# A decoder step on one core: state products in four row ranges, feed-forward without marking products, another closing chain, and new constants for the planner

## The chip, the cores and the metric

The kernel runs on one core of a Trainium2 chip, as one launch. The metric is the device time of that launch in microseconds (us); lower is better. The engines named below are TensorE (PE: matrix products; PEld is its weight load), VectorE (DVE), ScalarE (ACT), GpSimd (POOL) and SyncE (SP, which only issues DMAs). PE writes its products into PSUM, of which the kernel uses eight banks of 128 partitions by 512 fp32 values; its other tiles are in SBUF.

## The reference

One decoder layer is computed for 512 prompt tokens and for 8 x 4 sample tokens that share all weights; the kernel holds both as one block of N = 544 columns. In short:

```python
h = rmsnorm(x, norm_mix); z = h @ w_in            # attention q,k,v and HGRN q,f,i,g
f = lb + (1 - lb) * sigmoid(hf); qh = silu(hq) * HG_DK**-0.5
# HGRN, 4 heads of 128 x 128 state, causal; S0 = 0 for the prompt, given for each of the 8 samples
S_t = diag(f_t) S_{t-1} + (1 - f_t) outer i_t;  o_t = S_t^T qh_t
x = x + concat(att, o_normed_and_gated) @ w_out
x = x + cross_attention(rmsnorm(x)) @ w_co
u = rmsnorm(x, norm_ffn)
x = x + (silu(conv3(u @ w_gate)) * (u @ w_up)) @ w_down
y = rmsnorm(x, norm_final)
```

The outputs are y for prompt and samples, the new k and v rows, the HGRN states after the step, the last two gate rows and the memory keys and values.

## The kernel before, in words

**Numbers as pairs.** Nearly every large product runs on fp32r operands split into a high and a low part, three products for one (high x high, high x low, low x high). ACT makes the high parts, DVE the low ones. Small products (transposes, the HGRN state work, sums over partitions) stay in fp32, and each of those shows as two PE records.

**The recorder.** The kernel isn't issued as it is written. `Tape` records every call as a step with an estimated length (`_Engine.take`), its tiles and what it depends on; `Tape.order` then plays all engines forward in time and writes one fixed order for each engine. Steps recorded under `tape.main()` are the big products: they keep their written order on PE. All other PE work is side work, which the planner puts between them in bursts. The class constants (`BURST`, `PATIENCE`, `NEAR`, `SLACK`, `LEAD`, `MARGIN` and so on) say how eager it is, `EVEN` stretches the due times. Tiles of one kind share a pool (`a`: 71 SBUF tiles); a step can only be placed once its pool has room. The planner only orders instructions; on the chip nothing of it runs.

**PSUM.** Two banks are `dense` (`PD`), five are `aux` (`PX`), one is `dec` (`PDEC`); `PF` takes PD, PD, PDEC in turn.

**Stages, as the trace shows them.** Input projections and HGRN/attention as side work up to 307 us; output projection (`ps_wo`) to 355; cross attention to 428; feed-forward from 428 to about 730; the last third of the down projection (`ps_dz`, `ps_az`, `ps_cz`, `ps_ez`) to 786; closing norm and output after that.

**An HGRN head** (`hgrn`). `by_token_s` turns the 32 sample rows of v (into `psA`) and k (into `psin`) by a 128 x 32 product with the identity; two such copies go to partitions 0-31 and 32-63. ACT copies them to `hsm` (64 x 128). POOL spreads v into `hvm` (64 x 4 x 128), with `batch` as a mask. Two products with 32 rows and 512 columns, in two row ranges and two aux banks (`psu`), give the state updates of samples 0-3 and 4-7; eight DVE operations add each 128 x 128 part to the decayed state `hst`, which a DMA stores. `psU` and `psin` are aux banks that live around it; `pso` is the head's output, read by ACT as `ho`, normed, and used as `om` in the output projection.

**Feed-forward.** The gate and up projections run as `PLAIN` tiles (two gate, two up, columns cut 256 + 288 by `CUTS`) and then as 20 `Pair` units (Strassen/Winograd: seven products of 272 columns for two tiles, banks `a`, `c`, `d`). After product 1, ACT copies bank `a` into bank `d` (`keep`), and product 2 accumulates onto the copy. Before that, `mark_banks` (5 products) and `mark_down` (3 products) write 272 columns of each bank once. Products follow in the order 1, 3 of the unit before, 2, 6, 7, 4 of the unit before, 5; product 3 accumulates onto bank `a` after the copy `r` of product 5 has been read (`keptu` in the trace).

**Closing.** `last_half(7, 1)` makes the last 256 columns of the last feature tile: 30 products into `ps_dz`, a DVE add of `ps_dz` to x (`xr`), an ACT square (`sq_last`), then `final(1)`: sums over partitions (`psr_final`), ACT Ln (`r_fin`) and Exp (`r_final`), 8 scalings for each column cut (DVE or POOL) and 8 output DMAs for each, on SP for the first cut, on SP and ACT in turn for the second.

**Start.** The first DMAs are issued in written order: `vec` (norm weights) on ACT's queue; on SP's queue the first 256 columns of x, the first weights `wf[0]` in two pieces, the other columns of x, then x and weights in turn.

Of the kernel before, what the change touches and what calls it, by code (L numbers as in the profile page):

```python
# [12 lines left out]
AF = mybir.ActivationFunctionType  # L13
# [6 lines left out]
TS = 4  # L20
# [52 lines left out]
LAST_CUTS = ((0, 288), (288, 256))  # L73

# [21 lines left out]
for _n, _c in (("ident", 128), ("ones", 128), ("blk64", 128), ("dbias", NR + 2 * NS),  # L96
               ("mask_a", 96), ("mask_b", 96), ("mask_s", 96), ("batch", 4), ("sel32", 32), ("own", 2)):
    _span(CST_COLS, _n, _c)
# [17 lines left out]
def _constants():  # L116

    c = np.zeros((128, NCST), np.float32)

    def put(name, a):  # L120
        lo, hi = CST_COLS[name]
        c[:a.shape[0], lo:hi] = a.reshape(a.shape[0], hi - lo)

    p = np.arange(128)
    put("ident", np.eye(128))
    put("ones", np.ones((128, 128)))
    put("blk64", (p[:, None] // 64 == p[None, :] // 64).astype(np.float32))
# [27 lines left out]
    put("batch", ((p[:64, None] % 32 // TS) == 4 * (p[:64, None] // 32) + np.arange(4)[None, :]).astype(np.float32))  # L155
# [114 lines left out]
class Tape:  # L270
# [185 lines left out]
    def order(self):  # L456
# [16 lines left out]
        takes = sorted(takes.items(), key=lambda t: t[1])  # L473
        waiting = {e: [] for e in ("PE", "ACT", "DVE", "POOL", "SP")}
# [84 lines left out]
        def start(s):  # L559
            nonlocal todo, bus, mode  # L560
            waiting[s.engine].remove(s)
            for k, v in needs(s).items():
                room[k] -= v
            for n in s.tiles:
                if n in last and n not in held:
                    ends[n] = last[n]
# [19 lines left out]
            if s.main:  # L586
                clock[:] = s.est, now
            for n in s.tiles:
                if n in self.kinds:
                    left[n] -= 1  # L590
                    if not left[n]:
                        ends.pop(n, None)
                        frees.append((s.end + s.lag, self.kinds[n]))
# [70 lines left out]
class _Engine:  # L664
# [5 lines left out]
    def __getattr__(self, method):  # L670
# [3 lines left out]
        def take(*args, **kw):  # L674
# [10 lines left out]
            if engine == "PE":  # L685
                n, m, k = int(np.prod(args[2].shape[1:])), outs[0].shape[0], args[1].shape[0]
                codes = 2 if method == "transpose" or args[1].dtype == F32R else 4
                if method == "transpose":
                    n, length = 128, 0.11
                elif args[1].dtype == F32R:  # L690
                    length = 0.000456 * n + 0.001
                else:
                    least = 0.112 if m == 128 and k == 128 else 0.0105
                    length = 2 * max(least, 0.00086 * n * (max(m, 128 - 2 * k) / 128 if m < 128 else 1.0) * (0.59 if k <= 64 else 1.0))
                    length *= 0.5 if k <= 32 and m <= 32 else 1.0
# [3 lines left out]
            elif engine == "ACT":  # L699
                length = 0.05 + 0.00086 * n + 0.19 * ("accum_out" in kw)  # L700
                if hasattr(kw.get("bias"), "ap") or hasattr(kw.get("scale"), "ap"):
                    length += 0.13
# [6 lines left out]
            else:  # L709
                port = method == "tensor_tensor"  # L710
                length = {"tensor_tensor": 0.2 + 0.0026 * n, "memset": 0.15 + 0.0007 * n,
                          "tensor_scalar": 0.2 + 0.0036 * n}.get(method, 0.45 + 0.0009 * n)
# [5 lines left out]
def tile_decoder_step(ctx: ExitStack, tc: tile.TileContext, xT, memT, kwT, vw, s0, conv_in, mkT, mv, vecs, cst,  # L718
# [42 lines left out]
    nc.scalar.dma_start(vec[:, :KT], vecs[:, :KT])  # L761
# [158 lines left out]
    def passes(ps, w, xs, n0, n, order, first=True, last=True):  # L920
        for at, i in enumerate(order):
            (hi, lo), (xh, xl) = w[i], xs[i]
            for j, (a, b) in enumerate(((hi, xh), (hi, xl), (lo, xh))):
                nc.tensor.matmul(ps[:, :n], a, b[:, n0:n0 + n], start=(first and at == 0 and j == 0),
                                 stop=(last and at == len(order) - 1 and j == 2))
# [541 lines left out]
    def hgrn(h, f, q, gt, v):  # L1467
# [44 lines left out]
        def level_products(w, kq):  # L1512
# [8 lines left out]
            elif w == 32:  # L1521
                bank["l"] = PX(f"psL{h}")
                for c in range(4):
                    for j in (0, 64):
                        t0 = 128 * c + j
                        nc.tensor.matmul(bank["l"][j:j + 32, 128 * c + j + 32:128 * c + j + 64], kq[:, t0:t0 + 32],
                                         kq[:, t0 + 32:t0 + 64], start=True, stop=True)
            else:
                for c in range(4):
                    t0 = 128 * c  # L1530
                    nc.tensor.matmul(bank["l"][0:64, t0 + 64:t0 + 128], kq[:, t0:t0 + 64], kq[:, t0 + 64:t0 + 128],
                                     start=True, stop=True)

# [16 lines left out]
        vs, ks, ats = sml[:2 * NS, 0:128], sml[:2 * NS, 128:256], sml[:NS, 256:352]  # L1550
# [7 lines left out]
        for i in range(2):  # L1558

            by_token_s(v, bank["a"][NS * i:NS * i + NS, 384:512])  # L1560
# [11 lines left out]
        nc.scalar.copy(vs, bank["a"][:2 * NS, 384:512])  # L1572
# [8 lines left out]
        for i in range(2):  # L1581
            by_token_s(k, pin[NS * i:NS * i + NS, 256:384])
# [7 lines left out]
        nc.scalar.copy(ks, pin[:2 * NS, 256:384])  # L1590
        nc.vector.tensor_tensor(tmp[:, :384], tmp[:, :384], tmp2[:, :384], op=ALU.add)
        vm = A(f"hvm{h}", [128, 4, 128])
        nc.gpsimd.tensor_tensor(vm[:2 * NS], vs[:, None, :].to_broadcast([2 * NS, 4, 128]),
                                C("batch")[:2 * NS, :, None].to_broadcast([2 * NS, 4, 128]), op=ALU.mult)
# [8 lines left out]
        U, pus = PX(f"psU{h}"), [PX(f"psu{h}{i}") for i in range(2)]  # L1603
# [541 lines left out]
    def plain_tile(kind, j, i):  # L2145
# [9 lines left out]
        for cut in CUTS:  # L2155
# [200 lines left out]
    class Pair:  # L2356


        def __init__(self, kind, j, gates):
            self.name, self.w, self.s, self.low = f"{kind}{j}", {"A11": {}, "A12": {}}, {}, {}  # L2360
            src = w_gate if kind == "g" else w_up

# [47 lines left out]
        def product(self, bank, a, b, first, *deps):  # L2410
            def fn():
# [3 lines left out]
                for k in range(4):  # L2415
                    (hi, lo), (xh, xl) = w[k], xs[k]
                    for i, (l, r) in enumerate(((hi, xh), (hi, xl), (lo, xh))):
                        nc.tensor.matmul(ps[:, :HT], l, r, start=first and k == 0 and i == 0, stop=k == 3 and i == 2,
                                         skip_group_check=True)
            return later.pe(fn, self.low[a], tok_low[b, 0], tok_low[b, 1], *deps)  # L2420

        def keep(self, name, q):
            def fn():
                if name == "q":
                    out = self.s["d"] = PX(f"ps_d{self.name}")
# [48 lines left out]
    def mark_banks():  # L2474


        for i in range(5):
            nc.tensor.matmul(PX(f"ps_mark{i}")[:, :HT], ux[0][0][:, :128], ux[0][0][:, :HT], start=True, stop=True)

    later.pe(mark_banks)  # L2480
    later.pe(lambda: ffn_in.rows(1))
    seq[1:1] = [later.order.pop(), later.order.pop()]
    before = None

    def mark_down():

        for ps in (PD("ps_mark_a"), PD("ps_mark_d"), PDEC("ps_mark_c")):
            nc.tensor.matmul(ps[:, :HT], b_side("B11")[0][0][:, :128], b_side("B11")[0][0], start=True, stop=True)
# [33 lines left out]
    def last_half(m, c):  # L2522
# [309 lines left out]
```

## Time and profile before

| what | value |
|---|---|
| median of 3 runs | 799.51 us (799.26 to 799.98) |
| profiled execution | 798.79 us |
| its span, first to last instruction | 797.0 us |
| granted TensorE clock | 0.996 |
| PE busy | 784.1 us (98%), 7440 products |
| DVE / ACT / POOL busy | 673.9 / 480.1 / 206.6 us |
| HBM traffic | 142.9 MB (134.80 read, 8.07 written) |

The profiled execution's own time is 1.8 us above its span, and 0.7 us below the median of the runs. A PE record lasts from issue to the end of the pipeline, so records overlap: the time that a product costs is read from its start to the start of the next one, not from its duration.

### The profile page before, as it was taken

Reading aid. Unit: us, or ns where it says so; the run is one execution under the profiler, and the core shown is the slowest. Engines: PE = TensorE matmul, PEld = TensorE weight load, DVE = VectorE, ACT = ScalarE, POOL = GpSimd, SP = SyncE. Lnnn points to the kernel's source line nnn. Section 1 sums busy time; section 2 is a strip of 40 time slices with the busy share of each in tenths; the row PEclk is TensorE's granted clock in tenths of the full one; section 3 lists DMA queues with packets and bytes.
Section 4 is the critical chain, followed back from the end, with each engine's and each line's share of the span. In section 5 each row is a group of like instructions: output and inputs, shape, how many; then the busy total and the mean of one; then the engine's idle time right before and its main releaser. Section 6 shows DMA issues by size and latency. Waiting matters only on the chain.

```text
span 797.0 us, 19226 instructions
## 1 busy us (share of the span) xinstructions
PE 784.1 (98%) x7440; PEld 742.0 (93%) x7440; DVE 673.9 (85%) x1507; ACT 480.1 (60%) x1040; POOL 206.6 (26%) x284
## 2 busy tenths in 40 slices
PE   9999999999999999999999999999999999999995
PEld 9998878887898989999999999999999999999994
DVE  6889888578978886674888999999999998989963
ACT  8724468826558545553685767656665766567642
POOL 1131200030211110231234337423532433232023
PEclk9999999999999999999999999999999999999998
DMA  9753897799652364441754467877968877786103
GB/s 306 260 147 103 282 322 223 261 353 305 207 203 80 109 215 153 132 147 52 255 165 119 83 173 177 188 177 199 186 159 192 204 160 186 185 240 158 52 1 112
DMA packets 107419, 144.12 MB, mean 181 GB/s; under 512 B 7360, under 2 KB 73920, under 8 KB 107328
## 3 DMA queue, kind: packets, MB, share of 16 engines
q1 hardware_dynamic: 91728, 124.01, 48.3%
q0 software_dynamic: 14880, 18.36, 14.5%
q8 instruction: 58, 0.95, 0.5%
q10 hardware_dynamic: 720, 0.53, 0.2%
q14 instruction: 33, 0.27, 0.1%
HBM read 134.80 MB, written 8.07 MB: 179 GB/s over the span
## 4 chain that ended last, share of the span: by engine, by line
PE 97%; ACT 1%; DVE 1%; issue 0%; DVEq 0%; ACTq 0%
PE ps_ag L713 7%; PE ps_au L713 7%; PE ps_wo L713 6%; PE ps_aw L713 5%; PE ps_cu L713 4%; PE ps_cg L713 4%; PE ps_q L713 3%; PE ps_co L713 3%; PE ps_cq L713 3%; PE ps_first L713 3%; PE ps_dz L713 3%; PE ps_az L713 3%; PE ps_hv L713 2%; PE ps_cw L713 2%; PE ps_dg L713 2%; PE ps_ck L713 2%
## 5 line engine op out<-in xcount | busy, mean ns | idle before, releaser
L713 DVE TENSOR_TENSOR wl<-wr,wh 128x512 fp32r<-128x512 f32 x98 | 69.5, 733 | 3.3 <-ACT wh L713 3.2
L713 ACT CAST wh<-wr 128x512 fp32r<-128x512 f32 x98 | 56.3, 618 | 11.9 <-DMA wr<-in_w_in 6.1
L713 POOL TENSOR_TENSOR hG<-hG,hf 128x256 f32<-128x256 f32 (+1 forms) x28 | 25.1, 897 | 134.4 <-DVE hf L713 79.5
L713 POOL COPY last<-ug 128x2 f32<-128x2 f32 (+1 forms) x44 | 31.9, 788 | 59.0 <-DVE ug L713 56.4
L713 DVE SCALAR_TENSOR_TENSOR cv<-ug,vec,cv 128x560 f32<-128x560 f32 x44 | 35.2, 800 | 1.6 <-ACT cv L713 1.1
L684 POOL DMA_DIRECT2D S13w<-in_w_down x12 | 12.2, 1013 | 61.3 <-DVE ug L713 8.3
L713 POOL TENSOR_TENSOR acc_cx<-acc_cx,sq_cx 128x256 f32<-128x256 f32 (+1 forms) x14 | 12.6, 904 | 56.7 <-PE ps_wo L713 30.7
L713 ACT COPY keptg<-ps_ag 128x272 f32<-128x272 f32 x20 | 7.7, 386 | 28.9 <-PE ps_ag L713 28.9
L713 ACT ACTIVATE cv<-ug,vec 128x560 f32<-128x560 f32 x22 | 18.9, 858 | 4.7 <-POOL ug L713 3.5
L713 DVE TENSOR_TENSOR xr<-xr,ps_wo 128x256 f32<-128x256 f32 (+1 forms) x16 | 6.8, 436 | 15.1 <-PE ps_wo L713 15.1
L713 ACT ACTIVATE cv<-cv 128x560 f32<-128x560 f32 x22 | 14.8, 671 | 7.7 <-DVE cv L713 7.5
L713 PE MATMUL ps_co<-coh,wh 128*128 128x256 f32 (+1 forms) x64 | 19.0, 297 | 0.0
L713 POOL TENSOR_TENSOR acc_final<-acc_final,sq_final 128x256 f32<-128x256 f32 (+1 forms) x10 | 8.2, 834 | 40.2 <-ACT sq_final L713 40.1
L713 PE MATMUL ps_co<-coh,wl 128*128 128x256 f32 (+1 forms) x64 | 18.4, 288 | 0.0
L713 PE MATMUL ps_co<-col,wh 128*128 128x256 f32 (+1 forms) x64 | 18.4, 288 | 0.0
L713 POOL COPY ug<-conv_state 128x16 f32<-128x16 f32 x22 | 17.9, 992 | 0.0
L713 ACT ACTIVATE P<-P,mx 128x128 f32<-128x128 f32 (+3 forms) x32 | 17.6, 553 | 0.2
L713 ACT COPY hsm<-psA 64x128 f32<-64x128 f32 x4 | 1.0, 258 | 26.0 <-PE psA L713 17.7
L713 POOL MEMSET hG<- 128x544 f32 x4 | 2.2, 550 | 56.0 <-PE psr_att L713 45.9
L713 DVE TENSOR_TENSOR xr<-xr,ps_aw 128x272 f32<-128x272 f32 x36 | 15.6, 433 | 0.8 <-PE ps_aw L713 0.5
L713 DVE TENSOR_TENSOR hf<-hf 128x256 f32<-128x256 f32 (+1 forms) x28 | 12.2, 435 | 4.8 <-POOL hG L713 4.5
L713 PE MATMUL psd<-st,qbd_win 128*32 128x224 f32 x256 | 16.0, 358 | 0.0
(3348 smaller groups left out, 3812.7 us busy)
## 6 DMA issues: line engine op xcount, KB each, us to landing
st<-in_kwT SPq DMA_DIRECT2D x32, 448.0 KB, 5.6
st<-in_vw SPq DMA_DIRECT2D x28, 512.0 KB, 5.5
wr<-in_w_in SPq DMA_DIRECT2D x25, 512.0 KB, 6.6
wrg<-in_w_gate SPq DMA_DIRECT2D x10, 512.0 KB, 5.7
wru<-in_w_up SPq DMA_DIRECT2D x10, 512.0 KB, 4.8
st<-in_mkT SPq DMA_DIRECT2D x8, 512.0 KB, 5.4
wr<-in_w_out SPq DMA_DIRECT2D x8, 512.0 KB, 3.7
S13w<-in_w_down SPq DMA_DIRECT2D x24, 128.0 KB, 3.2
```

The source lines that it names most:

```text
L684: return tape.put(engine, lambda: call(*args, **kw), outs, ins, 0.1, 0.3, size)
L713: return tape.put(engine, lambda: call(*args, **kw), outs, ins, length, lag, size, port, codes, work, mode)
```

## The change

**State update of a head.** `by_token_s` runs four times for v and four times for k, into four 32-row ranges; `hsm`'s parts become 128 x 128, the mask `batch` has two columns, and POOL writes `hvm` as 128 x 2 x 128. Four products of 32 rows and 256 columns, in four row ranges and four aux banks, take the place of two of 512. The DVE work stays, reading other banks.

**Feed-forward.** Both marking steps go. The first three units write bank `d` once with one product at the end of product 1, and the last two plain tiles are cut 272 + 272. In the last unit product 7 goes behind product 5.

**Closing.** For the last feature tile ACT copies x into the PSUM bank ahead of the products, which accumulate onto it; ACT squares the bank directly, and DVE copies it to x.

**Start.** `wf[0]` goes to ACT's queue ahead of the table load; `vec` goes to SP's queue behind the first piece of x.

**Recorder.** New constants and lengths, and the planner now hands out a bank of a pool in the order in which banks are given back.

```diff
+HALVES = ((0, N // 2), (N // 2, N // 2))
+MARKED = 3
...
-    ROUNDS, EVEN = 2, 1.013
+    ROUNDS, EVEN = 2, 1.017
-    SWITCH, NEAR = 0.14, 3.9
-    SPELL, ACTIVE, IDLE, COLD = 3.4, 0.45, 0.45, 2.0
-    BURST, PATIENCE, SLACK, LEAD, MARGIN = 1.75, 3.7, 16.5, 15.95, 4.95
+    SWITCH, NEAR = 0.16, 3.25
+    SPELL, ACTIVE, IDLE, COLD = 3.4, 0.46, 0.45, 2.0
+    BURST, PATIENCE, SLACK, LEAD, MARGIN = 1.9, 5.85, 15.65, 14.75, 3.65
...
-            return all(room[k] >= v for k, v in want.items()) and ("a" not in want or leaves_room(s, want["a"]))
+            return all(room[k] >= v if k == "a" else len(give[k]) >= v and max(give[k][:v]) <= now + 1e-9
+                       for k, v in want.items()) and ("a" not in want or leaves_room(s, want["a"]))
...
-    nc.scalar.dma_start(vec[:, :KT], vecs[:, :KT])
...
+        for c0, c1 in ((0, 128), (128, 384)):
+            nc.scalar.dma_start(wf[0][:, c0:c1], w_first[0][:, c0:c1])
         nc.scalar.preload_act_table_set(LN_SET)
         x_load(0, 0, 256)
-        for c0, c1 in ((0, 128), (128, 384)):
-            nc.sync.dma_start(wf[0][:, c0:c1], w_first[0][:, c0:c1])
+        nc.sync.dma_start(vec[:, :KT], vecs[:, :KT])
         x_load(0, 256, N)
...
-        for i in range(2):
-
+        for i in range(4):
             by_token_s(v, bank["a"][NS * i:NS * i + NS, 384:512])
...
-        for i in range(2):
+        for i in range(4):
             by_token_s(k, pin[NS * i:NS * i + NS, 256:384])
...
-        vm = A(f"hvm{h}", [128, 4, 128])
+        vm = A(f"hvm{h}", [128, 2, 128])
...
-        U, pus = PX(f"psU{h}"), [PX(f"psu{h}{i}") for i in range(2)]
+        U, pus = PX(f"psU{h}"), [PX(f"psu{h}{j}") for j in range(4)]
...
-        for i in range(2):
-            rows = slice(NS * i, NS * i + NS)
-            nc.tensor.matmul(pus[i], ks[rows], vm[rows].rearrange("p b v -> p (b v)"), start=True, stop=True)
+        for j in range(4):
+            rows = slice(NS * j, NS * j + NS)
+            nc.tensor.matmul(pus[j][:, :256], ks[rows], vm[rows].rearrange("p b v -> p (b v)"), start=True, stop=True)
...
-                                               pus[i][:, 128 * j:128 * j + 128], op0=ALU.mult, op1=ALU.add)
+                                               pus[j][:, 128 * i:128 * i + 128], op0=ALU.mult, op1=ALU.add)
...
-        for cut in CUTS:
+        for cut in CUTS if i < ffn_w + 2 else HALVES:
...
+                if first and bank == "a" and self.mark:
+                    self.s["d"] = PX(f"ps_d{self.name}")
+                    nc.tensor.matmul(self.s["d"][:, :HT], w[0][0], xs[0][0], start=True, stop=True)
...
-    later.pe(mark_banks)
...
-    later.pe(mark_down, tok_low["B11", 0])
-    marks = later.order.pop()
...
-        if u == 1:
-            seq.append(marks)
-        for i in (1, 3, 2, 6, 7, 4, 5):
+        for i in (1, 3, 2, 6, 4, 5, 7) if unit is units[-1] else (1, 3, 2, 6, 7, 4, 5):
...
+        if m == KT - 1:
+            nc.scalar.copy(ps[:, :n], x[m][:, cut])
         with tape.main():
-            passes(ps, held[m], hs, n0, n, range(k))
-        add_to(m)(ps, n0, n)
+            passes(ps, held[m], hs, n0, n, range(k), copied=m == KT - 1)
         if m < KT - 1:
+            add_to(m)(ps, n0, n)
             ssq3.add(x[m][:, cut], n0, nc.vector if m == KT - 2 else None)
         else:
-            nc.scalar.activation(last_sq[:, cut], x[m][:, cut], AF.Square)
+            nc.scalar.activation(last_sq[:, cut], ps[:, :n], AF.Square)
+            nc.vector.tensor_copy(x[m][:, cut], ps[:, :n])
```

More of the change, by code (lines that the diff above doesn't have):

```diff
@@ L96 @@
 for _n, _c in (("ident", 128), ("ones", 128), ("blk64", 128), ("dbias", NR + 2 * NS),
-               ("mask_a", 96), ("mask_b", 96), ("mask_s", 96), ("batch", 4), ("sel32", 32), ("own", 2)):
+               ("mask_a", 96), ("mask_b", 96), ("mask_s", 96), ("batch", 2), ("sel32", 32), ("own", 2)):
     _span(CST_COLS, _n, _c)
@@ L154, in _constants @@
     put("mask_s", np.stack([level(w) for w in (0, 1, 2)], 1).astype(np.float32))
-    put("batch", ((p[:64, None] % 32 // TS) == 4 * (p[:64, None] // 32) + np.arange(4)[None, :]).astype(np.float32))
+    put("batch", (p[:, None] % 32 // TS == 4 * np.arange(2)[None, :] + p[:, None] // 32).astype(np.float32))
     put("sel32", (p[:, None] % 32 == np.arange(32)[None, :]).astype(np.float32))
@@ L473, in order @@
         takes = sorted(takes.items(), key=lambda t: t[1])
+        give, over = {k: [0.0] * n for k, n in room.items()}, {}
         waiting = {e: [] for e in ("PE", "ACT", "DVE", "POOL", "SP")}
@@ L563, in start @@
                 room[k] -= v
+                if k != "a":
+                    del give[k][:v]
             for n in s.tiles:
@@ L587, in start @@
                 clock[:] = s.est, now
+            gone = []
             for n in s.tiles:
@@ L590, in start @@
                     left[n] -= 1
+                    over[n] = max(over.get(n, 0.0), s.end + s.lag)
                     if not left[n]:
                         ends.pop(n, None)
-                        frees.append((s.end + s.lag, self.kinds[n]))
+                        frees.append((over[n], self.kinds[n]))
+                        gone.append((over[n], self.kinds[n]))
+            for t, k in sorted(gone):
+                give[k].append(t)
             todo -= 1
@@ L688, in take @@
                 if method == "transpose":
-                    n, length = 128, 0.11
+                    n, length = 128, 0.1
                 elif args[1].dtype == F32R:
@@ L692, in take @@
                 else:
-                    least = 0.112 if m == 128 and k == 128 else 0.0105
+                    least = 0.112 if m == 128 and k == 128 else 0.0093
                     length = 2 * max(least, 0.00086 * n * (max(m, 128 - 2 * k) / 128 if m < 128 else 1.0) * (0.59 if k <= 64 else 1.0))
-                    length *= 0.5 if k <= 32 and m <= 32 else 1.0
+                    length *= 0.5 if k <= 32 and (m <= 32 or n == 256) else 1.0
                 work = n * (1 if method != "transpose" and args[1].dtype == F32R else codes) / 2400.0 * m * k / 16384
@@ L699, in take @@
             elif engine == "ACT":
-                length = 0.05 + 0.00086 * n + 0.19 * ("accum_out" in kw)
+                length = 0.06 + 0.0009 * n + 0.12 * ("accum_out" in kw)
                 if hasattr(kw.get("bias"), "ap") or hasattr(kw.get("scale"), "ap"):
-                    length += 0.13
+                    length += 0.09
                 if method == "preload_act_table_set" or kw.get("func", args[2] if len(args) > 2 else None) == AF.Sigmoid:
@@ L917, in tile_decoder_step, with passes @@
     stream = Stream()
-    def passes(ps, w, xs, n0, n, order, first=True, last=True):
+    def passes(ps, w, xs, n0, n, order, first=True, last=True, copied=False):
         for at, i in enumerate(order):
@@ L923, in passes @@
             for j, (a, b) in enumerate(((hi, xh), (hi, xl), (lo, xh))):
-                nc.tensor.matmul(ps[:, :n], a, b[:, n0:n0 + n], start=(first and at == 0 and j == 0),
-                                 stop=(last and at == len(order) - 1 and j == 2))
+                nc.tensor.matmul(ps[:, :n], a, b[:, n0:n0 + n], start=(first and not copied and at == 0 and j == 0),
+                                 stop=(last and at == len(order) - 1 and j == 2), skip_group_check=copied)
     def half(w, xs, name, evac, cut, order=None):
@@ L1527, in level_products @@
                                          kq[:, t0 + 32:t0 + 64], start=True, stop=True)
+                tape.cur.length += 0.14
             else:
@@ L1532, in level_products @@
                                      start=True, stop=True)
+                tape.cur.length += 0.22
         v4 = lambda t: t[:, :384].rearrange("p (l c t) -> p l c t", l=3, c=4)
@@ L1549, in hgrn @@
         tmp, tmp2, sml = A(f"htm{h}"), A(f"htn{h}"), A(f"hsm{h}")
[L1550 removed]
+        vs, ks, ats = sml[:, 0:128], sml[:, 128:256], sml[:NS, 256:352]
         nc.vector.tensor_tensor(v4(tmp), v4(bank["b"]), m4(C("mask_b")), op=ALU.mult)
@@ L1571, in hgrn @@
         nc.vector.tensor_tensor(q[:, :N], q[:, :N], f[:, :N], op=ALU.mult)
-        nc.scalar.copy(vs, bank["a"][:2 * NS, 384:512])
+        nc.scalar.copy(vs, bank["a"][:, 384:512])
         nc.vector.tensor_tensor(v4(tmp2), v4(bank["a"]), m4(C("mask_a")), op=ALU.mult)
@@ L1589, in hgrn @@
         nc.scalar.copy(kt[:, :512], psk)
-        nc.scalar.copy(ks, pin[:2 * NS, 256:384])
+        nc.scalar.copy(ks, pin[:, 256:384])
         nc.vector.tensor_tensor(tmp[:, :384], tmp[:, :384], tmp2[:, :384], op=ALU.add)
-        vm = A(f"hvm{h}", [128, 4, 128])
-        nc.gpsimd.tensor_tensor(vm[:2 * NS], vs[:, None, :].to_broadcast([2 * NS, 4, 128]),
-                                C("batch")[:2 * NS, :, None].to_broadcast([2 * NS, 4, 128]), op=ALU.mult)
+        vm = A(f"hvm{h}", [128, 2, 128])
+        nc.gpsimd.tensor_tensor(vm, vs[:, None, :].to_broadcast([128, 2, 128]),
+                                C("batch")[:, :, None].to_broadcast([128, 2, 128]), op=ALU.mult)
         nc.vector.tensor_tensor(ats[:, :32], ats[:, :32], ats[:, 32:64], op=ALU.add)
@@ L2361, in __init__ @@
             src = w_gate if kind == "g" else w_up
+            self.mark = (kind, j) in PAIRS[:MARKED]
             def load():
@@ L2424, in fn @@
                 if name == "q":
-                    out = self.s["d"] = PX(f"ps_d{self.name}")
+                    out = self.s["d"] if self.mark else PX(f"ps_d{self.name}")
+                    self.s["d"] = out
                 elif name == "z":
@@ L2472, in tile_decoder_step @@
     seq.insert(-1, units[0].q.pop(1))
-    def mark_banks():
-        for i in range(5):
-            nc.tensor.matmul(PX(f"ps_mark{i}")[:, :HT], ux[0][0][:, :128], ux[0][0][:, :HT], start=True, stop=True)
-    later.pe(mark_banks)
     later.pe(lambda: ffn_in.rows(1))
-    seq[1:1] = [later.order.pop(), later.order.pop()]
+    seq.insert(1, later.order.pop())
     before = None
-    def mark_down():
-        for ps in (PD("ps_mark_a"), PD("ps_mark_d"), PDEC("ps_mark_c")):
-            nc.tensor.matmul(ps[:, :HT], b_side("B11")[0][0][:, :128], b_side("B11")[0][0], start=True, stop=True)
-    later.pe(mark_down, tok_low["B11", 0])
-    marks = later.order.pop()
     for u, unit in enumerate(units + [None]):
         q, b = unit.q if unit else {}, before.q if before else {}
-        if u == 1:
-            seq.append(marks)
-        for i in (1, 3, 2, 6, 7, 4, 5):
+        for i in (1, 3, 2, 6, 4, 5, 7) if unit is units[-1] else (1, 3, 2, 6, 7, 4, 5):
             s = b if i in (3, 4) else q
```

4 lines of the change are left out of this document (2 added, 2 removed).

## The prediction

> **What bounds the kernel now.** I read the page first, then PE's waits, then the timeline at each place that the change touches. The busy line and the chain that ended last:
>
> ```profile
> PE 784.1 (98%) x7440; PEld 742.0 (93%) x7440; DVE 673.9 (85%) x1507; ACT 480.1 (60%) x1040; POOL 206.6 (26%) x284
> PE 97%; ACT 1%; DVE 1%; issue 0%; DVEq 0%; ACTq 0%
> ```
>
> PE is busy for 98% of the span and carries 97% of the chain. An edit pays only if PE has less to issue, if a wait of PE goes, or if the start or the tail, where PE isn't the bound, gets shorter. Less DVE, ACT or POOL work pays nothing by itself. These are all waits of PE (us in total, times, longest):
>
> ```profile
> PE ps_first L713 <- DVE zero L713: 1.1, 1, 1.1
> PE ps_au L713 <- ACT keptu L713: 0.9, 1, 0.9
> PE psds L713 <- ACT ho L713: 0.7, 1, 0.7
> PE psr_final L713 <- ACT sq_last L713: 0.5, 1, 0.5
> PE ps_ak L713 <- ACT keptk L713: 0.5, 1, 0.5
> PE psA L713 <- issue: 0.2, 1, 0.2
> ```
>
> They sum to 3.9 us. That is nearly all that a better order could win by removing waits; the edits aim at the second and fourth.
>
> **State products.** The two products of the first and of the third head, each with the row behind it (start, us, engine, what; two records a product):
>
> ```profile
> 63.25 1.13 PE L713 MATMUL psu<-hvm,hsm 32*128 32x512 f32 x4
> 64.21 0.30 PE L713 MATMUL psin<-hsm 32*128 32x32 f32 x2
> ...
> 240.80 1.13 PE L713 MATMUL psu<-hvm,hsm 32*128 32x512 f32 x4
> 241.86 0.50 PE L713 MATMUL psr_att<-rh_att,sums 128*128 128x512 f32 x1
> ```
>
> Start to next start is 0.96 and 1.06 us, 1.0 in the mean. Four records that each last 0.6 us and more would take longer one by one, so the two row ranges run together, and 512 columns set the time. If four ranges run together too, 256 columns set it: at best 0.5 us saved a head, 2.0 in four. If only two at a time run together, twice 0.5 us is nothing saved. I take 1.75, near the first end, because the rows show two ranges that don't slow each other, less a little for the drain behind the last record, which isn't halved.
>
> The Trainium skill weighs in for a smaller gain: "TensorE: Matmul & The Clock Gate", Part 3, "Measured speedup vs the span model", gives 3.07 times for four 32-row tiles, not 4. Four products would then take 1.30 times one product's 0.5 us; as an estimate 0.35 us saved a head, 1.4 in all, and the sum below would be 0.35 us higher. No row here has four row ranges.
>
> **Four copies for two.** The change adds two turns of v and two of k a head, 16 in all. Nearest rows:
>
> ```profile
> 228.19 0.42 PE L713 MATMUL psin<-cs,hk 128*32 128x128 f32 x4
> 228.41 0.31 PE L713 MATMUL psS<-cs,v 128*32 128x128 f32 x2
> ...
> 290.82 0.65 PE L713 MATMUL psin<-hst,hq 128*32 128x128 f32 x16
> 291.40 0.50 PE L713 MATMUL ps_cv<-wh,mmh 128*128 128x512 f32 x1
> ```
>
> Two copies take 0.22 us. One behind another, eight more pairs would cost 1.75 us. In four column ranges, eight products of the same shape (16 records) take 0.58 us, so four take 0.29: 0.07 more a set, 0.6 in eight sets. I take 0.6, the row of the same shape in four ranges; ends 0.1 (wholly beside the first two) and 1.75. POOL's mask product shrinks, and ACT's copies keep their number of columns; neither is on the chain.
>
> **Marks.** The steps that go, each with its successor:
>
> ```profile
> 432.01 1.01 PE L713 MATMUL ps_mark<-ux0h 128*128 128x272 f32 x5
> 432.86 0.29 PE L713 MATMUL ps_g<-ux0h,wh 128*128 128x288 f32 x1
> ...
> 461.62 0.28 PE L713 MATMUL ps_mark_a<-B11h 128*128 128x272 f32 x1
> ...
> 461.99 0.29 PE L713 MATMUL ps_au<-B11h,A11u2h 128*128 128x272 f32 x1
> ```
>
> The three marks (`a`, `d`, `c`) take 0.37 us up to the next product, so 0.125 each. The five take 0.85, but the first has the change from fp32 in it, which the next product then pays. Eight go and three come back: 5 x 0.125 = 0.63 us saved, with PE dense on both sides and so at full price. Cutting two tiles 272 + 272 moves no column. Bank `d` of three units is held one product longer; three to four of five aux banks are then in use, so I cost that at nothing (a wait there would be at most one product of 1.5 us).
>
> **Last unit.** The wait is this:
>
> ```profile
> 725.31 0.85 ACT L713 ACTIVATE cv<-ug,vec 128x560 f32<-128x560 f32 x1
> 726.06 0.36 ACT L713 COPY keptu<-ps_au 128x272 f32<-128x272 f32 x1
> 726.48 0.39 PE L713 MATMUL ps_au<-B22h,S4u20h 128*128 128x272 f32 x1 [0.88 <-ACT keptu L713]
> ```
>
> Product 3 waits 0.88 us for a copy that stands behind another ACT operation. Product 7 in between is 12 x 0.125 = 1.5 us of cover; cv and the copy need 1.2. I take 0.9 saved. Next late would be product 4, which needs DVE's difference of bank `c` behind product 7; product 3 gives DVE 1.5 us for it. Ends: 0 (DVE's queue is longer than that) and 0.9.
>
> **Start.** The first data (PE, then ACT with what it waited for, then SP's issues):
>
> ```profile
> 3.66 0.55 PE L713 MATMUL ps_first<-xm0h,wfh 128*128 128x256 f32 x1
> 7.82 0.27 PE L713 MATMUL ps_first<-xm1l,wfh 128*128 128x256 f32 x1
> 8.12 0.39 PE L713 MATMUL ps_first<-xm1h,wfl 128*128 128x256 f32 x1
> ...
> 3.06 0.51 ACT L713 ACTIVATE xm0h<-x,vec 128x256 fp32r<-128x256 f32 x1 [0.60 <-DMA vec<-in_vecs]
> 6.02 0.75 ACT L713 ACTIVATE xm1h<-x,vec 128x544 fp32r<-128x544 f32 x1 [0.48 <-DMA x<-in_xT]
> ...
> 1.18 0.90 SPq L684 DMA_DIRECT2D wf<-in_w_first  x2
> ```
>
> An issue costs 0.45 us on SP. Taking two `wf` issues from SP and putting `vec` there moves all later x and weights one issue earlier; ACT was still waiting for such data at 6.02, and PE's hole before 8.12 (0.2 us beyond the usual 0.12) hangs on it, so it goes, and a little of the pace behind it with it. Against it, `vec` is issued 0.45 us later, and ACT waited for it last: the first product may start up to 0.25 later. The table load also slides behind two issues; ACT sat idle for 0.60 us before 3.06, which I take as its cover. I take 0.3 saved; ends 0.6 saved and 0.25 lost.
>
> **Closing.** PE's last products, ACT's square, DVE's and SP's rows of the tail:
>
> ```profile
> 786.46 0.42 DVE L713 TENSOR_TENSOR xr<-xr,ps_dz 128x256 f32<-128x256 f32 x1 [3.11 <-PE ps_dz L713]
> 786.80 4.69 DVE L713 SCALAR_TENSOR_TENSOR y<-xr,vec,r_final 128x288 f32<-128x288 f32 x11
> ...
> 783.51 0.42 ACT L713 ACTIVATE r_final<-r_fin 128x288 f32<-128x288 f32 x1
> 786.91 0.42 ACT L713 ACTIVATE sq_last<-xr 128x256 f32<-128x256 f32 x1 [2.51 <-DVE xr L713]
> ...
> 787.33 6.18 SPq L684 DMA_DIRECT2D out_yT<-y  x12
> ```
>
> The square can start 0.45 us earlier, since DVE's add leaves its path. But the page's chain follows only the last computing instruction. SP issues 12 output DMAs without a break from 787.33, half a microsecond each, until 793.5, two microseconds after DVE's last scaling at 791.5. This stream starts with the first scaling of the first cut, which stands on DVE behind the add. The copy that takes the add's place is as long, so the stream starts and ends as before. I take 0. Ends: 0.1 lost, and 1.5 saved if the new order puts first-cut scalings ahead of the copy (`r_final` of that cut is there at 783.9, and DVE sits idle for 3.1 us): the stream then ends with DVE's last scaling and one issue, 2.0 less 0.5 earlier. ACT's copy into the bank has to come before the 30 products. I cost it at nothing, with the products of the tile before it as cover; without it, 0.4 us once, as long as the square.
>
> **New order.** Constants move the whole side work up to 307 us. What it can win there is the 0.7 and 0.5 us above and a little drain between bursts; it can lose as much. I take 0, ends 1.5 either way.
>
> **Sum.** -1.75 + 0.6 - 0.63 - 0.9 - 0.3 = -2.98 us on the span of 797.0. The execution's own time is 1.8 above its span, and the median 0.7 above that time; I carry the difference to the median: 799.51 - 2.98 = 796.5 us.
>
> **Rivals.** *Only two row ranges at a time.* Then 1.75 goes: 798.3, no change that can be told. For it: no row with four. Against: two at a time don't slow each other.
>
> *The tail is freed as well.* With 1.5 in the closing and the waits of 0.7 and 0.5 gone: 793.8. For it: DVE idle for 3.1 us with ready work. Against: the same kind of planner left it so.
>
> *The new order eats the gain*, by 3 us more drains and waits: 799.5, the same.
>
> *Slower: the fourth head waits for banks.* Four `psu` with `psin` are all five aux banks. Rows of the fourth head and its deadline:
>
> ```profile
> 289.77 1.13 PE L713 MATMUL psu<-hvm,hsm 32*128 32x512 f32 x4
> 292.89 0.61 PE L713 MATMUL pso<-hAT,hvt 128*128 128x128 f32 x4
> 308.51 0.28 PE L713 MATMUL ps_wo<-om3h,wh 128*128 128x256 f32 x1
> ...
> 290.85 1.41 DVE L713 SCALAR_TENSOR_TENSOR domn<-psdn,drec,dom 128x512 f32<-128x512 f32 x2
> 293.10 2.15 DVE L713 SCALAR_TENSOR_TENSOR hst<-hst,ftots,psu 128x128 f32<-128x128 f32 x8
> 305.73 0.72 DVE L713 TENSOR_TENSOR om3l<-ho,om3h 128x544 fp32r<-128x544 f32 x1
> ```
>
> `psu` couldn't start before `psdn` is read at 292.3, and `pso`, if put behind it, not before five of the eight `hst` operations: about 295.2 instead of 292.9. The head has 2.0 us to spare (306.45 to 308.5), so this alone costs 0.3. If the 5.5 us for which `psu` is held (289.8 to 295.25) come on top, the slip is 7.8 and the stall 5.8: 802.3. A slip over 6.6 us decides. Against: `pso` needs one bank and may go first, as nothing on PE waits for `hst`. The skill's "TensorEngine Tiling (Array Packing)", "Gotcha 1", says that row tiles need different PSUM banks, so that sharing isn't a way out; no run here shows it.
>
> **How the numbers follow.** Chances: forecast 0.50; tail freed 0.16; two ranges at a time 0.14; gain eaten 0.09; banks 0.11. 0.2% is 1.6 us, about what a measurement can tell: faster below 797.9, slower above 801.1. Faster: 0.50 + 0.16 and a fifth of the 0.14, 0.69; same 0.20; slower 0.11. The forecast alone is 795.2 to 797.8; with both neighbours the range is 793.0 to 800.0.
>
> **What would show it.** The start of the first `psu` to the next form: about 0.55 us (four together) or 1.0. No `ps_mark`. No wait on `keptu`. `psr_final` 0.45 us sooner after `ps_dz`, with SP's stream still ending the run. PE's waits up to 307 us at 1.5 or less. Wrong if PE waits appear at `ps_wo`, or bursts of side work cost more drains.

## The result and the profile after

| kernel | median | runs | ratio to before, 95% interval |
|---|---|---|---|
| before | 799.91 us (799.26 to 800.59) | 6 | |
| changed | 794.18 us (793.51 to 794.71) | 6 | 0.9929 [0.9916, 0.9942] |

The changed kernel is 5.7 us faster; 3.0 were forecast. The time lies inside the range, below the likeliest value and close to that of the rival whose tail is freed. The profiled execution took 793.91 us, with a span of 792.1. From the page of the changed kernel, the busy line and the chain that ended last:

```profile
PE 780.7 (99%) x7483; PEld 742.0 (94%) x7483; DVE 673.7 (85%) x1507; ACT 483.7 (61%) x1041; POOL 198.3 (25%) x284
PE 96%; DVE 2%; ACT 0%; issue 0%; DMA 0%; DVEq 0%; SPq 0%; ACTq 0%
```

PE is still the bound, and is busy for 3.4 us less, though it has 43 records more. All waits of PE in the changed kernel (us in total, times, longest):

```profile
PE ps_first L724 <- DVE zero L724: 1.1, 1, 1.1
PE psr_final L724 <- ACT sq_last L724: 0.5, 1, 0.5
PE ps_ak L724 <- ACT keptk L724: 0.5, 1, 0.5
PE ps_co L724 <- DVE xr L724: 0.2, 1, 0.2
PE ps_first L724 <- ACT xm0h L724: 0.2, 1, 0.2
PE ps_ag L724 <- ACT keptg L724: 0.2, 1, 0.2
```

The waits on `keptu` and on `ho` are gone, three of 0.2 are new, and the wait in the closing is as it was: 2.7 us against 3.9. So waits explain 1.2 us. The rest shows only in the steps from one start to the next. Here are the ends of the stage in which the state update stands, the first q product and the first `ps_wo`, before and then after:

```profile
30.98 0.28 PE L713 MATMUL ps_q<-xm0h,wh 128*128 128x256 f32 x1
...
306.74 0.28 PE L713 MATMUL ps_wo<-om0h,wh 128*128 128x256 f32 x1
```

```profile
31.30 0.28 PE L724 MATMUL ps_q<-xm0h,wh 128*128 128x256 f32 x1
...
302.29 0.28 PE L724 MATMUL ps_wo<-om0h,wh 128*128 128x256 f32 x1
```

I call this the mix stage: 275.76 us before, 270.99 after. Cutting the span at the first record of each stage in this way gives the whole difference of 4.85 us:

| stage | before | after | difference |
|---|---|---|---|
| start to first q product | 30.98 | 31.30 | +0.32 |
| mix stage, to `ps_wo` | 275.76 | 270.99 | -4.77 |
| `ps_wo` to first `ps_g` | 121.67 | 122.42 | +0.75 |
| `ps_g` to first `ps_ag` (plain tiles) | 22.51 | 22.00 | -0.51 |
| `ps_ag` to first `ps_dz` (pair units) | 278.68 | 278.32 | -0.36 |
| `ps_dz` to its last product | 56.54 | 56.42 | -0.12 |
| last `ps_dz` product to the end | 10.85 | 10.70 | -0.15 |

Nearly all of it is in one stage, where the forecast had 1.15 us. Summing the steps by the tile that each starts with shows what shrank there: `psu` 1.18 us, `psS` 1.06, `pso` 1.02, `psdo` 0.53, `pst_hk` 0.48, `psd` 0.35; `psin` grew by 0.59. Only `psu`, `psin` and the copies in `psA` belong to the state update. `psS` and `pso` have the same products before and after; they cost less for the way in which they fall on PE. Two places of before:

```profile
190.93 1.68 PE L713 MATMUL psS<-k,q 64*128 64x512 f32 x4
192.54 0.66 PE L713 MATMUL pst_hk<-cs,hk 128*128 128x128 f32 x4
...
294.23 0.39 PE L713 MATMUL pso<-hq,hS 128*128 128x128 f32 x2
295.29 0.66 PE L713 MATMUL psds<-cs,domn 128*128 128x128 f32 x4 [0.67 <-ACT ho L713]
```

and the corresponding ones of after:

```profile
187.83 1.13 PE L724 MATMUL psS<-k,q 64*128 64x512 f32 x4
188.89 0.41 PE L724 MATMUL psL<-kq 128*32 128x32 f32 x13
...
290.75 0.39 PE L724 MATMUL pso<-hq,hS 128*128 128x128 f32 x2
290.98 0.39 PE L724 MATMUL psr_attS<-dsq,sums 128*128 128x128 f32 x2
```

The same four `psS` records take 1.61 us to the next start before and 1.06 after. In the records behind these rows, after's four run in two pairs (starts 7, 526, 7 and 519 ns apart), while in before only the middle two ran together (533, 21, 533, 520). The last two `pso` records take 1.06 against 0.23: before, the next product waited for ACT.

### The profile page after: what moved, and what is told of

It is laid out like the page before. It is cut to its first block, busy times and chain, and to the rows that moved or that the text cites. A ratio compares the mean times of both kernels' runs of the same rounds, so it can differ in the third digit from the quotient of the medians.

```text
span 792.1 us, 19317 instructions
## 1 busy us (share of the span) xinstructions
PE 780.7 (99%) x7483; PEld 742.0 (94%) x7483; DVE 673.7 (85%) x1507; ACT 483.7 (61%) x1041; POOL 198.3 (25%) x284
## 4 chain that ended last, share of the span: by engine, by line
PE 96%; DVE 2%; ACT 0%; issue 0%; DMA 0%; DVEq 0%; SPq 0%; ACTq 0%
PE ps_au L724 7%; PE ps_ag L724 7%; PE ps_wo L724 6%; PE ps_aw L724 5%; PE ps_cu L724 4%; PE ps_cg L724 4%; PE ps_q L724 3%; PE ps_cq L724 3%; PE ps_dz L724 3%; PE ps_co L724 3%; PE ps_first L724 3%; PE ps_az L724 3%; PE ps_hv L724 2%; PE ps_cw L724 2%; PE ps_du L724 2%; PE ps_ck L724 2%
## 5 line engine op out<-in xcount | busy, mean ns | idle before, releaser
L724 POOL COPY last<-ug 128x16 f32<-128x16 f32 (+1 forms) x44 | 30.8, 779 | 60.9 <-DVE ug L724 59.6
L724 DVE CUSTOM_DVE_ANT_0 P<-psS,bias 128x128 f32<-128x128 f32 (+3 forms) x32 | 14.1, 485 | 1.1 <-PE psS L724 1.0
```

The costliest lines, as they stand in the source:

```text
L724: return tape.put(engine, lambda: call(*args, **kw), outs, ins, length, lag, size, port, codes, work, mode)
```

## The experiments

The theory after the result: most of the gain comes from the new order, which the prediction had at nothing. The rivals: the state update, or another part, is worth more than its own rows show. The kernels below undo one part or do one alone. Every comparison is with runs of before on the same chip, whose median moved from 798.72 to 800.27 us between chips, so times from different chips compare through the ratio.

**Only the planner, and all but the planner.**

```diff
plan_only: before with
+    ROUNDS, EVEN = 2, 1.017
+    SWITCH, NEAR = 0.16, 3.25
+    BURST, PATIENCE, SLACK, LEAD, MARGIN = 1.9, 5.85, 15.65, 14.75, 3.65
... the new lengths and the new rule for handing out banks
all_but_plan: the changed kernel with these undone
```

> The kernel before with only the new planner: its constants, lengths and the order in which banks come free. The changed kernel gained 4.8 us between the first query projection and the output projection, where the prediction had 1.15. Theory 1 (the order): most of the other 3.6 us is the new order of the side work; this kernel then takes 796.5 to 797.5 us, with that stage 3 us shorter. Theory 2 (the state update): the gain comes from the state products and what they free, and the new planner alone gives nothing: 799 to 800.5 us.

> The changed kernel with the old planner: old constants, lengths and bank order, every other edit in. Theory 1 (the order): it keeps only the edits' own work, about 797 us (state 1.2, marks and last unit 1.0, closing 0.1, start lost 0.3). Theory 2 (the state update): 794 to 795 us, as the changed kernel.

`plan_only`: 796.16 us (795.35 to 796.31), 0.9953 [0.9940, 0.9967]. It issues exactly the products of before and is 3.6 us faster (0.3 below the first theory's range), with a mix stage of 272.84. The order alone gives over half of the gain. It also gives the loss between `ps_wo` and `ps_g` (122.40 us there).

`all_but_plan`: 808.82 us (807.36 to 809.8), 1.0114 [1.0100, 1.0128]. With every part of the change but the planner the kernel is 9 us slower than before; neither theory had that. Its mix stage takes 283.4 us. The timeline of PE at the fourth head:

```profile
271.52 0.66 PE L715 MATMUL pst_v<-cs,v 128*128 128x128 f32 x4
277.09 0.66 PE L715 MATMUL psA<-kq 128*32 128x32 f32 x32 [4.91 <-DVE kq L715]
...
279.17 0.42 PE L715 MATMUL ps_ck<-mml,wh 128*128 128x256 f32 x1
...
283.00 0.28 PE L715 MATMUL ps_ck<-mml,wh 128*128 128x256 f32 x1
```

and stretches of it (us, busy time and records of each engine, then granted clock, DMA share, GB/s):

```profile
265.00:271.00 6.00, 6.00 (x78) 4.82 (x77) 4.74 (x17) 5.94 (x19) 0.88 (x1) 1.00 0.12 46
271.00:277.00 6.00, 1.13 (x8) 0.65 (x7) 5.95 (x18) 6.00 (x18) 0.72 (x1) 0.93 0.00 0
...
279.00:283.00 4.00, 4.00 (x19) 4.00 (x20) 3.05 (x7) 0.53 (x2) 1.60 (x2) 0.50 0.53 167
```

PE stands still for 4.91 us because the operands `kq` come from DVE, which is busy for 5.95 of the 6 us there (third pair of numbers): the planner had put `psA` before DVE could reach its work. After the wait the granted clock is 0.50, and `ps_ck` products start 0.21 us apart instead of 0.12 until 282.8. Some twenty of them at 0.09 more are 1.9 us on top of the wait. The Trainium skill, "TensorE: Matmul & The Clock Gate", Part 1, states that at least one idle window of about 3.4 us halves the clock, and that it stays so until PE has been busy for at least one such window. This trace agrees: the clock is halved after 4.91 us without work, and the slow pace lasted 5.7 us from the restart. So the slow kernel is not the prediction's rival with the banks, for neither `psu` nor `pso` waited; but a stall that makes the changed kernel slower was possible, on another path.

**The new order, nudged.** If the gain belongs to the new constants as such, small shifts of a constant should keep it.

```diff
nudge_slack:  -SLACK = 15.65   +SLACK = 15.9
nudge_margin: -MARGIN = 3.65   +MARGIN = 3.9
```

> The changed kernel with one constant of the planner moved by 1.6 % (SLACK 15.65 to 15.9), which moves some 215 of TensorE's 5534 instructions, all before ps_wo. If the gain of the new order is a property of the new prices and rules: within 0.8 us of the changed kernel, 793.4 to 795.0. If the order was picked out of many with a scatter like that between the two kernels' orders: 795.5 to 799, lost between the first q product and ps_wo (271.0 us there in the changed kernel, 272.8 and more here), in new waits or drains of TensorE.

> The changed kernel with another constant moved by 7 % (MARGIN 3.65 to 3.9), which moves some 290 of TensorE's instructions before ps_wo. Same two readings as for SLACK: 793.4 to 795.0 if the gain belongs to the prices and rules, 795.5 to 799 if the order was a picked one. A stall of TensorE of some microseconds, as the one of 4.9 us in all_but_plan, would give 800 and more.

`nudge_slack`: 797.0 us (796.4 to 798.84), 0.9978 [0.9969, 0.9987]. `nudge_margin`: 798.05 us (797.08 to 799.8), 0.9992 [0.9983, 1.0001]: no gain is left that can be told, though every edit is in. The mix stages are 273.75 and 276.02 us. In `nudge_margin` a few waits of PE return, the longest this one, and `psB`, `psin` and `psS` cost 0.6 to 1.1 us more each:

```profile
PE psL L724 <- DVE kq L724: 1.4, 1, 1.4
```

Both times lie in the range of the second reading: the orders that two neighbouring constants give take 2.8 and 5.0 us longer in this stage, and the changed kernel has the shortest of the six that ran (`all_but_state` has that of `plan_only`). Two neighbours don't show how such orders are spread. The changed kernel's order also ran in the kernels below that undo other parts, so the table can say what one execution adds: 0.96 us between seven profiles of that order, 0.7 of it in `psd`, whose operand comes by DMA.

| order | mix stage, us |
|---|---|
| changed kernel (two profiles) | 270.99, 271.52 |
| its order in five other kernels | 271.18 to 271.94 |
| its order in `all_but_start`, with a wait of 0.9 for a late state | 272.58 |
| plan_only, all_but_state | 272.84, 272.66 |
| nudge_slack | 273.75 |
| before | 275.76 |
| nudge_margin | 276.02 |
| all_but_plan | 283.4 |

**Without the state update; without the feed-forward part.**

```diff
all_but_state: the changed kernel with
+        for i in range(2):            # two copies of v, two of k
+        U, pus = PX(f"psU{h}"), [PX(f"psu{h}{i}") for i in range(2)]
all_but_ffn: the changed kernel with
+    later.pe(mark_banks)
+    later.pe(mark_down, tok_low["B11", 0])
+        for i in (1, 3, 2, 6, 7, 4, 5):
```

> The changed kernel with the old state update (two products of 512 columns in two row ranges, two copies of v and k); its TensorE order up to ps_wo is then that of plan_only. Forecast of the prediction: the update with its copies is worth 1.15 us, so 794.2 + 1.15 = 795.3. By the rows of the changed kernel (psu 1.18 us less, psin and the v copies 0.8 more): 0.4 us, so 794.6. If the update also makes room for a better order (stage from the first q product to ps_wo 272.8 us in plan_only, 271.0 in the changed kernel): 796.0.

> The changed kernel with the old feed-forward (eight marking products, the last unit in the old order, tiles of 256 and 288 columns); TensorE's order up to ps_wo is unchanged. Forecast of the prediction: marks 0.63 and last unit 0.9, so 794.2 + 1.5 = 795.7. By the stages of the profiles shown so far (0.46 less up to ps_ag, 0.21 to 0.36 less up to ps_dz): 0.7 to 0.8, so 794.9 to 795.0. If the wait on the copied bank of the last unit is only replaced by waits at the three marking products: 0.5, so 794.7, with PE ps_au <- ACT keptu 0.9 back among the waits in each case.

`all_but_state`: 795.53 us (795.37 to 797.09), 0.9964 [0.9951, 0.9976]. Its mix stage is 1.67 us longer than that of the changed kernel's first profile, and 0.7 to 1.7 longer than in the seven of the table. That is the third reading, and by the ratios it is 2.8 us. By steps, `psu` costs 1.12 more and `psin` 0.51 less, so 0.6 is the update's own; the rest is the place of others, `pso` alone 1.29. Whether the update made room for that place, or this order only happens to have it, no run shows.

`all_but_ffn`: 796.05 us (795.51 to 797.93), 0.9971 [0.9961, 0.9981]. Up to `ps_wo` its order is that of the changed kernel, and the mix stage took 271.3. From `ps_g` to `ps_dz` it needs 301.36 us against 300.31: the part is worth 1.05. The ratios say 3.4, but in the profile 1.2 of the rest lies ahead of the first q product, where two profiles of the changed kernel differ by 1.06, and 0.3 in the mix stage. The `keptu` wait is back:

```profile
PE ps_au L722 <- ACT keptu L722: 0.8, 1, 0.8
```

By steps: `ps_au` 1.09 us less in the changed kernel, and the marks 1.22 less (0.85 for the five, 0.37 for the three). But the products that took over the marking give 1.19 back: `ps_du` and `ps_dg` 0.97, and `ps_g`, now the first behind the fp32 work, 0.22. One such place in the changed kernel:

```profile
458.88 0.29 PE L724 MATMUL ps_du<-B11h,A11u2h 128*128 128x272 f32 x1
459.33 0.39 PE L724 MATMUL ps_ag<-B22h,S4g2h 128*128 128x272 f32 x1 [0.16 <-ACT keptg L724]
```

It takes 0.45 us to the next start, where 0.125 was priced; a wait of 0.16 for the copy of the bank is half of the excess.

**Start and closing.**

```diff
all_but_start: the changed kernel with vec first on ACT's queue, wf[0] on SP's
all_but_close: the changed kernel with the DVE add, and the square behind it
tail_early: the changed kernel with
+        with tape.early(None if c else 120.0):   # Ln, Exp and the scalings of the first cut
tail_no_pool: tail_early with
-    ON_POOL = (1, 3, 6), (1, 5)
+    ON_POOL = (1, 3, 6), ()
tail_no_pool_old_start: tail_no_pool with the old start
after_again: the changed kernel
```

> The changed kernel with the old start: norm weights on ACT's queue, first weights on SP's; PE and DVE keep exactly the order of the changed kernel. Theory 1: the new start loses 0.3 to 0.4 us, because the norm weights that ACT waits for come last: 793.8 us, with the first product at 3.66 instead of 4.16 us. Rival: the later products are fed sooner and the early loss is made good: 794.2 us or more.

> The changed kernel with DVE's five first-cut scalings ahead of the copy of the last tile (the closing steps of the first cut get a long lead in the planner); PE and ACT keep their order. Theory 1 (SP's stream of output DMAs ends the run): the stream starts about 3 us sooner, and the run ends with DVE's last scaling and one issue: 1.3 to 1.8 us less, 792.4 to 792.9 us. Rival (the chain through the square and the sums ends it): no change, 794.2 us.

> The changed kernel itself, on the chip and beside the runs of before that the next three share: 0.993 of the time before, as in its own comparison (0.9916 to 0.9942). Its profile shows how much of a stage is the execution's and not the kernel's: the time up to ps_hv, 25.29 us in the first profile, may come out between 24.9 and 26.6, since other kernels with the same start did; every stage from the first q product to the end within 0.1 us of the first profile, unless a DMA comes late.

> The changed kernel with the old closing (the residual added by DVE behind the last 30 products, the square behind the add); TensorE's order is the same. Forecast of the prediction: the closing is worth 0 (ends 0.1 lost, 1.5 saved), so the time of after_again within 0.2 us, and psr_final's last products as late after the last ps_dz product as in the changed kernel. If the square had really moved ahead: 0.45 us slower than after_again.

> tail_early with the two scalings that GpSimd does in the second cut given to DVE. If what ends tail_early is GpSimd's drain (6.4 us from its last scalings in before, in the changed kernel and in tail_early alike): the end comes 0.7 to 1.0 us sooner after the last ps_dz product than in tail_early (10.05 us), so about 9.2, and some 1.4 us less than after_again. If SP's and ACT's stream of output DMAs ends it: DVE's two more scalings of 0.4 us each put it 0.4 to 0.8 later, 10.5 to 10.9.

> tail_no_pool with the old start (vec issued first on ACT, the first weights by SP). TensorE's order is the same. Forecast of the prediction: the new start is worth 0.3 us, so 0.3 slower than tail_no_pool. By the profiles shown so far (time up to ps_hv 24.96, 24.96 and 25.14 us with the old start in three kernels; 24.95 to 26.59, 25.56 in the mean of seven, with the new): 0.2 to 0.5 faster. If the 0.9 us for which TensorE waited on a late state in all_but_start belongs to the old start: 0.5 or more slower, with that wait back.

| kernel | median, us | ratio to before | time up to `ps_hv` | last `ps_dz` to end |
|---|---|---|---|---|
| all_but_start | 794.98 (794.49 to 795.8) | 0.9944 [0.9932, 0.9956] | 25.14 | 10.69 |
| after_again | 794.98 (794.14 to 796.5) | 0.9941 [0.9926, 0.9955] | 26.34 | 10.70 |
| all_but_close | 794.12 (793.88 to 795.58) | 0.9933 [0.9919, 0.9948] | 26.65 | 10.70 |
| tail_early | 793.91 (793.61 to 794.89) | 0.9932 [0.9919, 0.9944] | 25.24 | 10.05 |
| tail_no_pool | 792.73 (792.35 to 793.96) | 0.9912 [0.9897, 0.9928] | 26.35 | 8.66 |
| tail_no_pool_old_start | 792.83 (791.93 to 793.15) | 0.9910 [0.9895, 0.9925] | 24.85 | 8.68 |

*Start.* With the shortened tail in both, old and new start differ by 0.1 us, which is nothing that can be told. Nor can the other pair be told apart: 0.9944 with the old start, 0.9929 and 0.9941 with the new. The late state for which `all_but_start` stood 0.9 us in its profile did not come back with the old start, so it belonged to that execution. Two profiles of the changed kernel show what moves (PE, the first and then the second):

```profile
4.16 0.58 PE L724 MATMUL ps_first<-xm0h,wfh 128*128 128x256 f32 x1 [0.18 <-ACT xm0h L724]
...
7.31 0.65 PE L724 MATMUL ps_first<-xm0h,wfh 128*128 128x288 f32 x3
7.80 0.56 PE L724 MATMUL ps_first<-xm0l,wfh 128*128 128x288 f32 x3
```

```profile
4.28 0.58 PE L724 MATMUL ps_first<-xm0h,wfh 128*128 128x256 f32 x1 [0.29 <-ACT xm0h L724]
...
7.50 1.07 PE L724 MATMUL ps_first<-xm0h,wfh 128*128 128x288 f32 x3
8.36 0.92 PE L724 MATMUL ps_first<-xm0l,wfh 128*128 128x288 f32 x3
```

Three products of 288 columns take 0.49 us to the next start in the one and 0.86 in the other. The record of the granted clock in a trace begins with its step to full pace: at 7.25 us in the first profile, just ahead of these products, and at 9.47 in the second, behind them. (For the time before its first record a view prints 1.00.) Over the fourteen profiles the step lies between 4.43 and 10.10 us, and `ps_hv` follows it: reached at 24.85 to 25.30 us where the step comes by 7.25, at 26.34 to 26.65 where it comes at 9.47 or later. "TensorE: Matmul & The Clock Gate" of the Trainium skill, Part 1, states that the window which ends the slow pace runs freely, so that the count of slow products varies from run to run of one kernel. These two profiles agree, with the step 2.2 us apart. Of the ten profiles with the new start six have it at 7.25 or later, of the four with the old none. In the ten PE waits 0.18 to 0.30 us ahead of its first product, in the four it doesn't. Whether that hole delays the step stays open: four of the ten have an early step all the same, and the medians tell no difference.

*Closing.* The old closing in the changed kernel takes 10.70 us from the last `ps_dz` product, the new one 10.70, and the intervals overlap, though the median is 0.86 us below that of `after_again`, where 0.2 was expected. The tail of the changed kernel, DVE, ACT, PE and SP's queue:

```profile
781.76 0.42 DVE L724 COPY xr<-ps_dz 128x256 f32<-128x256 f32 x1 [3.11 <-PE ps_dz L724]
...
782.22 0.38 ACT L724 ACTIVATE sq_last<-ps_dz 128x256 f32<-128x256 f32 x1 [2.57 <-DVE xr L724]
...
782.65 0.70 PE L724 MATMUL psr_final<-sq_last,sums 128*128 128x256 f32 x2 [0.50 <-ACT sq_last L724]
...
782.63 6.00 SPq L695 DMA_DIRECT2D out_yT<-y  x12
```

The square no longer needs DVE's result, but it was ordered behind DVE's copy from the same bank and waits for it. So `psr_final` comes 1.21 us after the last `ps_dz` product, as before (1.24). In `tail_early` the planner placed the square first:

```profile
782.41 0.38 ACT L724 ACTIVATE sq_last<-ps_dz 128x256 f32<-128x256 f32 x1 [2.11 <-PE ps_dz L724]
...
782.83 0.42 DVE L724 COPY xr<-ps_dz 128x256 f32<-128x256 f32 x1 [0.76 <-ACT sq_last L724]
...
782.85 0.70 PE L724 MATMUL psr_final<-sq_last,sums 128*128 128x256 f32 x2
...
780.40 6.62 SPq L695 DMA_DIRECT2D out_yT<-y  x12
```

PE's wait is gone, and SP's stream starts 1.7 us ahead of the last `ps_dz` product instead of 1.2 behind it. Yet the end comes only 0.65 sooner, and the ratio, 0.9932 against 0.9929, shows no gain. What holds it is in the trace but in no view of the page: POOL's last drain, 6.39 us from 784.97, beside its last two scalings. In before it lasts 6.40 from 789.50, in the changed kernel 6.40 from 784.77, each time up to about 1 us ahead of the end. In all fourteen traces it ends 4.95 us after POOL's last operation. The other path is SP's: it waits for the output transfers to land, and its own drain ends at 791.38 in the changed kernel, 0.21 behind POOL's. In `tail_early` SP's ends at 790.26 and POOL's at 791.37, so there POOL holds the end. `tail_no_pool` takes POOL out of the second cut: its drain begins at 782.12 (6.89 us) and ends 2.3 us ahead of SP's. What ends the run now is DVE's last scalings and the output transfers that they release:

```profile
785.86 3.22 DVE L724 SCALAR_TENSOR_TENSOR y<-xr,vec,r_final 128x256 f32<-128x256 f32 x8 [1.26 <-ACT r_final L724]
...
781.75 7.30 SPq L695 DMA_DIRECT2D out_yT<-y  x12
```

The end comes at 8.66 us, 2.04 sooner than in the changed kernel and 1.39 sooner than in `tail_early`, although DVE works 0.8 us longer; 9.2 was expected. With either start this tail makes the best versions that ran, 0.9912 and 0.9910 of before; beside `after_again` on the same chip its median is 2.25 us lower.

## Why the prediction was right or wrong, step by step

That the time fell inside the range is in good part luck. The parts with a price were to give 2.98 us; their own work gives about 1.65 (0.6 in the state update, 1.05 in the feed-forward, nothing that can be told at the start). The rest of the 4.85 us in the span goes with the order, a term that stood at 0.

*New order, taken as 0 with ends of 1.5.* This step failed. `plan_only` measures it alone: 3.6 us gained in the medians, 2.6 in the span (2.9 in the mix stage, 0.7 lost behind `ps_wo`). The reasoning was that only two PE waits could be won. The waits were indeed small; what moved was the step of the same products beside other neighbours, which no list of waits holds. The ends were too narrow as well: the orders that ran span 5 us in that stage without a stall, 12 with one.

*State products, 1.75.* Four row ranges do run together; the rows of the second and the third head:

```profile
194.81 0.71 PE L724 MATMUL psu<-hvm,hsm 32*128 32x256 f32 x8
195.46 0.40 PE L724 MATMUL ps_hv<-xm0h,wh 128*128 128x288 f32 x1
...
232.81 0.97 PE L724 MATMUL psu<-hvm,hsm 32*128 32x256 f32 x8
233.71 0.40 PE L724 MATMUL ps_hq<-xm0h,wh 128*128 128x288 f32 x1
```

0.65 us to the next form in three heads, 0.90 in the third, where the fourth range lags by 0.26. The sum went from 4.01 to 2.83: 1.18, not 1.75. The drain behind the last record, for which the prediction took off 0.25 in all, does not account for that. In the records behind these rows the first four start within 0.02 us, and the second four follow 0.32 us after the first. `psS` in two 64-row ranges takes 0.22 us from one such set to the next at 256 columns, and 0.53 at 512. So the excess over half is in every set and comes with the four ranges; what sets it stays open. The ratio of 3.07 in the Trainium skill ("TensorE: Matmul & The Clock Gate", Part 3, "Measured speedup vs the span model"), set beside the forecast, gave 1.30 times 0.5, which is 0.65: the rows agree, except in the third head.

*Four copies, 0.6 lost.* Measured 0.5 (`psin`), with `psA` unchanged between `plan_only` and the changed kernel. Right. The update by itself is thus worth 0.6, not 1.15. Undoing it cost 1.67 in the stage, because the order changed with it.

*Marks, 0.63, and last unit, 0.9.* Together 1.05 instead of 1.53. The last unit was right, 1.09 with its wait gone. The marks gave nothing: 1.22 saved, 1.19 paid at their successors, where I had priced three returning products at 0.125 each.

*Start, 0.3.* Nothing that the runs can tell. The first product came 0.5 later in the first profile, twice the bound I had set: `vec` was issued later. The step of the clock to full pace, which the sum did not have, moved the time up to `ps_hv` by more than that.

*Closing, 0.* Right in the sum, for a reason that was half of the true one. The square did not move 0.45 sooner, and SP's path ended the run, but only 0.21 us behind a second one, POOL's drain, that I did not have.

*Rivals.* The time landed near the one of the freed tail, but the tail was not freed: 0.15 of 4.85 is there. Two row ranges at a time is refuted by the rows above. The banks of the fourth head are not seen in the changed kernel.

## What to carry to other kernels

When a change also moves an order that a program makes, time the new order alone on the old work, and a few of its neighbours, before crediting the edits: here one constant moved by 7 % took back the gain. Look for the cost of an order in the steps from start to start of the same products, not in the list of waits. And where the end of a run does not follow the stream that seems to set it, look for a second path that ends at the same time.

## What the runs showed of the hardware

- POOL's last drain ended 4.95 us after POOL's last operation in all fourteen traces. It held the end of `tail_early`, and moving POOL's last two scalings to DVE ended the run 1.39 us sooner.
- The granted clock stepped to full pace at 4.43 to 10.10 us into the span, at 7.25 and 9.47 in two profiles of the changed kernel; up to `ps_hv` that was worth 1.06 us between these two, and 1.7 between kernels with the same start.
- Four products in four 32-row ranges took 0.32 us from their first records to their second at 256 columns; two in two 64-row ranges took 0.22.
- One of four row ranges started 0.26 us late in one head of four, and cost the whole lag.
